# Second feed-forward product of a hybrid diffusion block: tokens on the output's partitions, weights as the moving side

## The chip, the cores and the metric

The kernel runs on one core of one Trainium2 chip. The metric is the device time of one execution in microseconds (us). A core has engines that work side by side and wait for each other through semaphores: TensorE (PE, matrix products; its weight loads are listed apart as PEld), VectorE (DVE), ScalarE (ACT), GpSimd (POOL) and SyncE (SP, which here only issues transfers). Transfers (DMAs) run on queues of their own, which share 16 DMA engines. [...]

In a matrix product one operand is *stationary*: PE loads a block of 128 x 128 of it ahead of the matmul. The other one is *moving*: up to 512 columns of it stream through. The stationary operand's columns become the partitions of the result, the moving operand's columns its free dimension.

## The reference

One layer of a diffusion block over 512 tokens of width D = 1024, with 256 context tokens beside them, in float32, and a last RMSNorm:

```python
h_lat = modulate(x, norm1_g[l], sh1, sc1)
h_ctx = modulate(ctx, norm1_g[l], csh1, csc1)
o_lat, o_ctx = token_mixer(h_lat, h_ctx, ...)      # Mamba-2 SSD and windowed attention, merged, one output product
x = x + gt1 * o_lat
x = x + gt2 * conv_ffn(modulate(x, norm2_g[l], sh2, sc2), w_up[l], ffn_conv_w[l], ffn_conv_b[l], w_down[l])
return rmsnorm(x, final_g)

def conv_ffn(h, w_up, conv_w, conv_b, w_down):
    u = dwconv_centred(h @ w_up, conv_w, conv_b)   # w_up: 1024 x 5632; 3 taps along the tokens
    a, b = u[..., :D_FF], u[..., D_FF:]            # D_FF = 2816
    return (jax.nn.silu(a) * b) @ w_down           # w_down: 2816 x 1024
```

`modulate` is an RMSNorm over the channels, times (1 + scale), plus shift; shift, scale and the gate gt2 are vectors over the channels. The change touches what comes after the first residual sum (called x1 below): the second feed-forward product `@ w_down` ("down"; `h @ w_up` is "up"), the second residual sum, the last RMSNorm and the store of the result.

## The kernel before, in words

**Layout.** The kernel keeps channels on partitions: x1 stands as eight tiles of 128 channels x 512 tokens (`x1[c // 4][:, c % 4, :]`), and so do the normalized input, the up product's tiles and the result, which is stored as (channels, tokens) and turned on the host. A per-channel vector (the gate, a norm's weight) is thus one value per partition; a sum over channels is one over partitions.

**Precision.** Each float32 operand is split into a high and a low part (`hi`, `lo`), and each product is three matmuls: hi by hi, hi by lo, lo by hi. Weights are split on the chip: `split` (L177) copies to `whi` on ACT (L178) and subtracts on DVE to `wlo` (L179).

**Weights.** The program is a list of steps that `run` (L201) goes through; each names the weight pieces it needs, and `run` calls `load` a fixed number of pieces ahead. `load_raw` (L164) issues the transfer on SP's queue into one of three buffers `wraw` of 128 x 1024 (for half of the down pieces into the larger `dnraw`). `weave` (L213) strews the steps of one list between those of another. A planner sets the order of the instructions on each engine by estimated times and priorities, except where a `manual_schedule` block or a `keep_in_program_order` holds it.

**Second norm and up product.** The tokens are handled in two halves of 256. In the first of 22 up steps (`up_step`, L1906) the normalized tiles of a half are made one after the other by `norm2_k` (L1844: DVE scales into `tb`, ACT makes the high part `mh`, DVE or POOL the low part `ml`), and PE uses each (L1915) as soon as it is there. In every later step `gemm` (L228, L229, L231) makes two tiles of 128 channels x 512 tokens, 24 matmuls of 512 moving tokens each; `up_first` and `up_second` apply the convolution and the gated SiLU into `F["x"]` (`fx`), and `f_sums` (L1867) makes the operands of the down product's first two products.

**Down product.** Down is a 2 x 2 block product by the scheme with seven products: the blocks are two halves of the tokens and two of the output channels, and the even and odd tiles of the 2816 inner channels. Its operands are sums and differences of blocks. Those of the weights are made by POOL's accumulating transfers in DRAM early on (`SUMS`, `DSUMS`); those of the activations by `f_sums`. Each product j has an operand `fs` of 11 tiles (DK = 11) x 256 tokens, hi and lo, and four column blocks q of 128 output channels. `product` (L1963) makes one: 11 x 3 matmuls (L1971 to L1973) with a weight block of 128 x 128 stationary and 256 tokens moving, on a half PSUM bank. Its weights come as two pieces of 768 and 640 columns. Products 0, 2 and 4 accumulate in one pair of banks (`mis`), the others in banks of their own (`acc`).

**Beside it.** `down_step` (L1977) adds what a column block gives to x1 at once: `x_add` (L1949) is one DVE operation with the gate as a per-partition value, `half_square` (L1954) squares a finished tile on ACT and adds it to `q3` on DVE. In products 1 to 5 `f_split` (L1863) splits the operand of the next product.

**The last product and the end.** `down_last` (L2014) handles the last RMSNorm. The sum over channels is made on PE (`rms_sums`, L271), then come DVE (L281) and POOL's power (L282), and the root is spread over the partitions by PE transposes (`rms_spread`, L288). For one half of the tokens (`u` = 1) this stands inside the last product's matmuls (`root`, `spread`, `early`), and `finish` (L2018) scales and stores it there; for the other half it comes after the last matmul (L2072, L2073, then `rms_root`, `rms_spread`, `finish`).

The order of steps is in the list handed to `run`: after `close_c1` come the 22 up steps, woven with what is left of the modulation's steps, then `down_step(j, q)` for 6 products of 4 column blocks, then `down_last()`.

Of the kernel before, what the change touches and what calls it, by code (L numbers as in the profile page):

```python
# [44 lines left out]
def tile_hybrid_layer(  # L45
# [25 lines left out]
    win_d: bass.AP,  # L71
    sel_d: bass.AP,
# [67 lines left out]
    DPARTS = ((0, 6), (6, DK - 6))  # L140
    DSUMS = {i: dpool.tile([4, P, DK * P], F32, name="dsum%d" % i) for i in (1, 2, 4, 5)}
    for q in range(4):
        for j, t in enumerate((wdn[0, q], DSUMS[1][q], DSUMS[2][q], wdn[1, q], DSUMS[4][q], DSUMS[5][q], wdn[3, q])):
            for u, (k0, n) in enumerate(DPARTS):
                src["dn", (4 * j + q) * 2 + u] = t[:, k0 * P : (k0 + n) * P], n * P

    SUMS = []
    for j, first_, more in (
        (4, wdn[0], wdn[2]), (1, wdn[2], wdn[3]), (2, DSUMS[4], wdn[3]), (5, DSUMS[2], wdn[1]),
    ):  # L150
        SUMS += [(DSUMS[j][q], first_[q], {}) for q in range(4)]
        SUMS += [(DSUMS[j][q], more[q], dict(accum_op=ALU.add, max_dma_last_dim=DK * P)) for q in range(4)]
# [11 lines left out]
    def load_raw(key):  # L164
        a, n = src[key]
        if key[0] == "dn" and key[1] >= 4 and key[1] % 2:
            if "dnraw" not in F:
                F["dnraw"] = hpool.tile([P, 5, 6 * P], F32, tag="hlh", name="dnraw")
            r = F["dnraw"][:, key[1] // 2 % 5, :]
        else:  # L170
            r = wpool.tile([P, 1024], F32, tag="raw", name="wraw", bufs=3)
# [11 lines left out]
    def load(key):  # L183
# [7 lines left out]
        if key[0] == "dn" and key[1] % 4 > 1:  # L191
            if "dnw" not in F:
                F["dnw"] = hpool.tile([P, 2, 2, 6 * P], F32R, tag="hll", name="dnw")
# [54 lines left out]
    a1 = cpool.tile([P, KT, 2], F32, name="a1")  # L248
    s1 = cpool.tile([P, KT, 2], F32, name="s1")
# [9 lines left out]
    tt_d = dpool.tile([64, 4], F32, name="tt_d")  # L259

# [138 lines left out]
    ssq = hpool.tile([P, L], F32, name="ssq")  # L399
# [1541 lines left out]
    q3 = hpool.tile([P, L], F32, tag="q2", name="q3")  # L1941

    ng2 = cpool.tile([P, 4], F32, name="ng2")
# [5 lines left out]
    def x_add(c, u, a, ps):  # L1949
        x = x1[c // 4][:, c % 4, HALF[u]]  # L1950
        g = ng2[:, c - 4 : c - 3] if a < 0 else mod2[:, 24 + c : 25 + c]
        V.scalar_tensor_tensor(x, ps, g, x, ALU.mult, ALU.add)

    def half_square(c, u):  # L1954
        x, q = x1[c // 4][:, c % 4, HALF[u]], q3[:, HALF[u]]
        if c % 4 == 0 and (c, u) in ((0, 0), (4, 1)):
            S.activation(q, x, AF.Square)
        else:
            sq = tmp("tc")[:, :HL]
            S.activation(sq, x, AF.Square)  # L1960
            V.tensor_tensor(q, q, sq, ALU.add)

    def product(j, q, w, ps, st, after={}):  # L1963
        s = F["s"][(0, 1, 0, 1, 0, 1, 0)[j]]
        with tc.manual_schedule(engines={mybir.EngineType.PE}):
            for u, (k0, n) in enumerate(DPARTS):
                wh, wl = w[u]
                for k in range(n):
                    c, h, l = slice(k * P, (k + 1) * P), s[:, 0, k0 + k, :], s[:, 1, k0 + k, :]
                    en = k0 + k == DK - 1  # L1970
                    T.matmul(ps, wh[:, c], h, start=st and k0 + k == 0, stop=False, skip_group_check=True)  # L1971
                    T.matmul(ps, wh[:, c], l, start=False, stop=False, skip_group_check=True)  # L1972
                    T.matmul(ps, wl[:, c], h, start=False, stop=en, skip_group_check=True)  # L1973
                    if k0 + k in after:
                        after[k0 + k]()

    def down_step(j, q):  # L1977
        def fn(*w):
            if j == 0 and q == 0:
                V.tensor_scalar_mul(ng2, mod2[:, 28:32], -1.0)  # L1980
# [198 lines left out]
```

## Time and profile before

| | |
|---|---|
| median of 3 runs | 1230.14 us (1230.03 to 1231.89) |
| profiled execution, its own time | 1229.7 us |
| span from first to last instruction | 1227.9 us |
| granted TensorE clock, mean | 0.998 |
| first and last matmul of the down product start | 1106.5 and 1218.4 us |
| DMA packets | 104,761, with 206.35 MB |

The page of a profile gives, in this order: busy time, share of the span and number of instructions of each engine; the span in 40 slices, a digit of tenths of busy time for each engine; the DMA queues; the chain of work that ended last, followed back from the end; and the costliest groups of instructions. A group's row names line, engine, operation, output <- inputs, their shapes and the count, then total busy time and the mean of one in ns, then the idle time just ahead of them with what ended it. A row of the timeline has the start in us, the length, engine, line, operation and shapes; in brackets, how long the engine was idle ahead of it and what released it. Matmuls overlap in the pipe: a matmul's length is longer than its distance to the next one.

### The profile page before, as it was taken

Reading aid. Unit: us, or ns where it says so; the run is one execution under the profiler, and the core shown is the slowest. Engines: PE = TensorE matmul, PEld = TensorE weight load, DVE = VectorE, ACT = ScalarE, POOL = GpSimd, SP = SyncE. Lnnn points to the kernel's source line nnn. Section 1 sums busy time; section 2 is a strip of 40 time slices with the busy share of each in tenths; the row PEclk is TensorE's granted clock in tenths of the full one; section 3 lists DMA queues with packets and bytes.
Section 4 is the critical chain, followed back from the end, with each engine's and each line's share of the span. In section 5 each row is a group of like instructions: output and inputs, shape, how many; then the busy total and the mean of one; then the engine's idle time right before and its main releaser. Section 6 shows DMA issues by size and latency. Waiting matters only on the chain.

```text
span 1227.9 us, 18427 instructions
## 1 busy us (share of the span) xinstructions
PE 1218.8 (99%) x6790; PEld 1021.5 (83%) x6790; DVE 921.4 (75%) x1518; ACT 686.7 (56%) x1289; POOL 170.0 (14%) x177
## 2 busy tenths in 40 slices
PE   9999999999999999999999999999999999999997
PEld 6798888888878878778777778889988888889997
DVE  5857788888555598797896767676777777778785
ACT  5658788787545367485574763223634434345662
POOL 0000120100000043252542540000200000000000
PEclk9999999999999999999999999999999999999999
DMA  9755799744754446356366568676233433337662
GB/s 368 256 136 185 156 257 259 161 153 129 177 158 143 129 103 183 120 120 196 106 169 208 164 212 282 206 242 206 58 116 104 136 114 110 117 102 236 187 178 82
DMA packets 104761, 206.35 MB, mean 168 GB/s; under 512 B 8928, under 2 KB 52768, under 8 KB 104416
## 3 DMA queue, kind: packets, MB, share of 16 engines
q1 hardware_dynamic: 94736, 181.32, 48.1%
q0 software_dynamic: 8960, 23.07, 8.2%
q8 instruction: 53, 0.87, 0.3%
q10 hardware_dynamic: 976, 0.79, 0.2%
q14 instruction: 36, 0.29, 0.1%
HBM read 182.54 MB, written 40.17 MB: 181 GB/s over the span
## 4 chain that ended last, share of the span: by engine, by line
PE 99%; DVE 0%; ACT 0%; issue 0%; POOL 0%; DVEq 0%; ACTq 0%; POOLq 0%
PE acc L228 20%; PE acc L231 20%; PE acc L229 20%; PE score L946 3%; PE po L995 3%; PE pt L982 2%; PE mis L568 2%; PE mis L1599 2%; PE mis L1492 2%; PE acc L1971 2%; PE acc L1973 2%; PE acc L1972 2%; PE mis L1607 1%; PE mis L1972 1%; PE mis L1971 1%; PE mis L1973 1%
## 5 line engine op out<-in xcount | busy, mean ns | idle before, releaser
L178 ACT CAST whi<-wraw 128x1024 fp32r<-128x1024 f32 (+3 forms) x118 | 120.0, 1018 | 156.4 <-PE acc L229 112.1
L228 PE MATMUL acc<-hlh,whi 128*128 128x512 f32 x472 | 194.2, 411 | 0.0
L179 DVE TENSOR_TENSOR wlo<-wraw,whi 128x1024 fp32r<-128x1024 f32 (+3 forms) x118 | 142.9, 1211 | 66.6 <-ACT whi L178 63.4
L229 PE MATMUL acc<-hll,whi 128*128 128x512 f32 x472 | 185.0, 392 | 0.0
L231 PE MATMUL acc<-hlh,wlo 128*128 128x512 f32 x472 | 184.8, 392 | 0.0
L228 PE MATMUL acc<-mh,whi 128*128 128x512 f32 x368 | 143.3, 390 | 0.0
L229 PE MATMUL acc<-ml,whi 128*128 128x512 f32 x368 | 143.2, 389 | 0.0
L231 PE MATMUL acc<-mh,wlo 128*128 128x512 f32 x368 | 143.2, 389 | 0.0
L231 PEld LDWEIGHTS acc<-hlh,wlo 128*128 128x128 f32 x472 | 88.6, 188 | 19.5
L228 PEld LDWEIGHTS acc<-hlh,whi 128*128 128x128 f32 x472 | 88.8, 188 | 18.0 <-issue 3.1
L229 PEld LDWEIGHTS acc<-hll,whi 128*128 128x128 f32 x472 | 89.0, 188 | 17.3 <-issue 2.4
L231 PEld LDWEIGHTS acc<-mh,wlo 128*128 128x128 f32 x368 | 69.1, 188 | 14.5
L229 PEld LDWEIGHTS acc<-ml,whi 128*128 128x128 f32 x368 | 69.1, 188 | 14.3
L228 PEld LDWEIGHTS acc<-mh,whi 128*128 128x128 f32 x368 | 69.1, 188 | 14.2
L282 POOL TENSOR_TENSOR rs<-ms,phalf 128x2 f32<-128x2 f32 (+1 forms) x5 | 4.8, 955 | 463.2 <-DVE ms L281 463.2
L1380 DVE SCALAR_TENSOR_TENSOR ta<-acc,half,ta 128x511 f32<-128x511 f32 (+1 forms) x66 | 43.9, 665 | 27.8 <-ACT ta L1379 27.6
L955 DVE CUSTOM_DVE_ANT_0 p<-score,winm,nsink 128x512 f32<-128x512 f32 (+1 forms) x64 | 51.9, 810 | 15.4 <-PE score L946 13.9
L1379 ACT ACTIVATE ta<-acc,half 128x512 f32<-128x512 f32 (+1 forms) x66 | 46.8, 709 | 22.3 <-PE acc L231 21.0
L962 ACT ACTIVATE p<-p,mneg 128x512 f32<-128x512 f32 (+1 forms) x64 | 49.7, 777 | 15.4 <-DVE mneg L955 14.8
L228 PE MATMUL acc<-hch,whi 128*128 128x256 f32 x176 | 54.7, 311 | 0.0
L990 DVE TENSOR_TENSOR ptl<-pt,pth 128x512 fp32r<-128x512 f32 x72 | 47.5, 685 | 8.5 <-ACT pth L986 7.7
L784 DVE SCALAR_TENSOR_TENSOR tm<-wraw,csil,tm 128x512 f32<-128x512 f32 x56 | 44.4, 793 | 12.4 <-DMA wraw<-wm 11.3
(414 smaller groups left out, 3160.6 us busy)
## 6 DMA issues: line engine op xcount, KB each, us to landing
wraw<-wup SPq DMA_DIRECT2D x44, 512.0 KB, 3.5
dsum<-wdn POOLq DMA_DIRECT2D x24, 704.0 KB, 8.6
fb<-cs_d SPq DMA_DIRECT2D x32, 512.0 KB, 6.5
wraw<-wm SPq DMA_DIRECT2D x32, 512.0 KB, 3.7
wraw<-wx SPq DMA_DIRECT2D x24, 512.0 KB, 3.6
wm<-wm SPq DMA_DIRECT2D x16, 512.0 KB, 8.4
wraw<-wz SPq DMA_DIRECT2D x16, 512.0 KB, 4.1
wraw<-wos SPq DMA_DIRECT2D x16, 512.0 KB, 4.6
```

The lines of the kernel that those rows point to most:

```text
L178: S.copy(hi[:, :n], r[:, :n])
L179: return V.tensor_tensor(lo[:, :n], r[:, :n], raw(hi[:, :n]), ALU.subtract)
L228: T.matmul(ps, wh, xh[:, k0 + k, :], start=a, stop=False)
L229: T.matmul(ps, wh, xl[:, k0 + k, :], start=False, stop=False)
L231: T.matmul(ps, wl, xh[:, k0 + k, :], start=False, stop=b)
L784: V.scalar_tensor_tensor(acc, r[:, u * 512 : u * 512 + 512], sc, acc, ALU.mult, ALU.add)
L946: T.matmul(ps[:, o : o + len(z) * P], Q[h][:, b * P : (b + 1) * P], k[:, j, z[0] * P : (z[-1] + 1) * P], start=v == 0 and o % 512 in (0, P ...
L955: V.tensor_tensor_reduce(p[:, :w], d["ps"][i][:, o0 : o0 + w], m, op0=ALU.add, op1=ALU.min, scale=1.0, scalar=nsink[:, h : h + 1], accum_o ...
L962: S.activation(p, p, AF.Exp, bias=d["mneg"][:, i : i + 1], scale=-1.0, accum_out=d["den"][:, i : i + 1])
L990: V.tensor_tensor(d["ptl"][x], d["pt"][x], raw(d["pth"][x]), ALU.subtract)
L1379: S.activation(o[:, :n], ps[:, :n], AF.Identity, scale=hcol(base_w, stride + i), bias=hcol(base_b, i))
L1380: V.scalar_tensor_tensor(o[:, 1:n], ps[:, 0 : n - 1], hcol(base_w, i), o[:, 1:n], ALU.mult, ALU.add)
```

## The change

The down product is turned: its result has tokens on the partitions. Of an activation operand `fs` a block of 128 tokens is stationary, and 512 weight columns (half of the output channels) are moving. Each of the seven products then has two blocks of 128 tokens instead of four of 128 channels, with 11 x 3 matmuls each on a full PSUM bank. The scheme, its sums and the number of weights are the same.

- **Weights.** `wdn` is packed so that for each inner tile its 512 columns are next to each other. A product's weights are loaded as six pieces (DU = 6), five of 1024 columns (two inner tiles) and one of 512, instead of eight of 768 or 640. `DSUMS` has the same layout; its transfers stay 24 + 8 of the old sizes. `dnraw` has 4 buffers of 1024 instead of 5 of 768.
- **x1 is turned through DRAM.** `x1_turn(c)`, eight times: a DVE transpose within blocks of 32 x 32 of x1's tile c into a buffer `te`, then four SP transfers that write it to `x1_d` (tokens, channels) in DRAM, each of 512 runs of 32 values (128 bytes). `x1_load` then reads x1 back as four tiles of 128 tokens x 1024 channels. These steps are woven into the up steps.
- **Row tiles.** The gate and the last norm's weight now run along the free dimension. `row_tiles` makes tiles of 128 x 512 of them by broadcasting transfers from DRAM (`g2_d`, written there first in pieces of 4 bytes, and `fg_d`, a new input).
- **Sums.** `x_add` and `half_square` go. The functions in `BESIDE_DOWN` take their place, each at one step (j, u): copies of PSUM on ACT, sums on DVE, multiplication by the gate and the residual sum on POOL, all 512 wide. Squares are summed along the free dimension by ACT's `accum_out`; the sums, spreads and transposes of the last norm on PE go.
- **The end.** The last step of the last product takes two weight pieces and does block 0's nine matmuls, then block 1's nine. `near_last` and `near_out` do the rest for each block; the scaled rows are stored as (tokens, channels), so nothing is turned on the host.

```diff
     DK = NFF // 2
-    DPARTS = ((0, 6), (6, DK - 6))
+    HC = D // 2
+    DU = (DK + 1) // 2
...
+    for j, t in enumerate((wdn[0], DSUMS[1], DSUMS[2], wdn[1], DSUMS[4], DSUMS[5], wdn[3])):
+        for u in range(DU):
+            n = min(2, DK - 2 * u) * HC
+            src["dn", DU * j + u] = t[:, 1024 * u : 1024 * u + n], n
...
-                F["dnraw"] = hpool.tile([P, 5, 6 * P], F32, tag="hlh", name="dnraw")
+                F["dnraw"] = hpool.tile([P, 4, 1024], F32, tag="hlh", name="dnraw")
...
+    def x1_turn(c):
+        def fn():
+            t = tmp("te")
+            V.transpose(t, x1[c // 4][:, c % 4, :])
+            for a in range(4):
+                o = x1_d[:, c * P + 32 * a : c * P + 32 * a + 32].rearrange("(f i) j -> i f j", i=32)
+                nc.sync.dma_start(o, t[32 * a : 32 * a + 32, :].rearrange("i (f j) -> i f j", j=32))
+        return [], fn
+
+    def x1_load():
+        F["xt"] = []
+        for h, tag in enumerate(("hch", "hcl")):
+            x = hpool.tile([P, 2, D], F32, tag=tag, name="xt")
+            F["xt"].append(x)
+            for i in range(2):
+                r = 256 * h + P * i
+                nc.sync.dma_start(x[:, i, :], x1_d[r : r + P, :])
...
+    def row_tiles():
+        V.tensor_copy(g2c[:, 0:4], mod2[:, 24:28])
+        V.tensor_scalar_mul(g2c[:, 4:8], mod2[:, 28:32], -1.0)
+        nc.sync.dma_start(g2_d.rearrange("(c p) -> p c", p=P), g2c)
+        tiles = [hpool.tile([P, HC], F32, tag=t, name="row" + t) for t in ("q2", "ssq", "rbc4")] + [tmp("tm")]
+        rows_["g"], rows_["f"] = tiles[:2], tiles[2:]
+        for i in range(2):
+            z = slice(HC * i, HC * i + HC)
+            nc.sync.dma_start(rows_["f"][i], fg_d[z].partition_broadcast(P))
+            nc.sync.dma_start(rows_["g"][i], g2_d[z].partition_broadcast(P))
...
+    def square_sum(h, i, col_, x):
+        sq = tmp("ta")[:, : x.shape[-1]]
+        S.activation(sq, x, AF.Square, scale=1.0 / 32.0, accum_out=ss[:, 2 * h + i, col_ : col_ + 1])
+
+    def scale_add(x, y, g, h, i, c):
+        G.tensor_tensor(x, y, rows_["g"][c], ALU.mult)
+        G.tensor_tensor(xq(h, i, c), xq(h, i, c), x, ALU.add)
...
+    def near_last(i):
+        ps = F["ps", 6][i]
+        for b, z in enumerate(HALF):
+            t = tmp("ta")[:, :HL]
+            V.tensor_tensor(t, ps[:, z], rows_["g"][1][:, z], ALU.mult)
+            x = xq(0, i, 1, z)
+            V.tensor_tensor(x, x, t, ALU.add)
+            square_sum(0, i, 1 + b, x)
+        F["near", i] = mean_root(0, i, ss[:, i, 1:2], ss[:, i, 2:3], ss[:, i, 0:1])
+
+    def near_out(i):
+        rs, r = F["near", i], P * i
+        S.activation(F["p1"][i], F["p1"][i], AF.Copy, scale=rs)
+        S.dma_start(out[r : r + P, 0:HC], F["p1"][i])
+        for z in HALF:
+            x = xq(0, i, 1, z)
+            V.scalar_tensor_tensor(x, x, rs, rows_["f"][1][:, z], ALU.mult, ALU.mult)
+            nc.sync.dma_start(out[r : r + P, HC + z.start : HC + z.stop], x)
+
+    BESIDE_DOWN = {
+        (0, 0): row_tiles, (1, 0): first_kept, (2, 0): fifth_kept, (3, 0): far_sum, (4, 0): near_sum, (4, 4): near_done,
+        (5, 0): lower_sums, (5, 5): lower_done, (6, 0): upper_sums, (6, 3): lambda: (upper_done(), far_roots()),
+    }
...
-                    T.matmul(ps, wh[:, c], h, start=st and k0 + k == 0, stop=False, skip_group_check=True)
-                    T.matmul(ps, wh[:, c], l, start=False, stop=False, skip_group_check=True)
-                    T.matmul(ps, wl[:, c], h, start=False, stop=en, skip_group_check=True)
...
+                wh, wl = (x[:, k % 2 * HC : k % 2 * HC + HC] for x in w[k // 2])
+                h, l = s[:, 0, k, tok], s[:, 1, k, tok]
+                st, en = k == 0 and (j == 0 or not chain), k == DK - 1
+                T.matmul(ps, h, wh, start=st, stop=False, skip_group_check=True)
+                T.matmul(ps, l, wh, start=False, stop=False, skip_group_check=True)
+                T.matmul(ps, h, wl, start=False, stop=en, skip_group_check=True)
...
+        tail = j == 6 and u == DU - 2
...
+            if tail:
+                far_out()
+                for i in TWO:
+                    product(j, i, w, ks)
+                with tc.manual_schedule(engines={mybir.EngineType.DVE, mybir.EngineType.Activation}):
+                    for f in (near_last, near_out):
+                        for i in TWO:
+                            f(i)
+                return
+            for k in ks:
+                for i in TWO:
+                    product(j, i, w, (k,))
...
-        + weave([up_step(t) for t in range(NFF)], msteps[24:])
-        + [down_step(j, q) for j in range(6) for q in range(4)]
-        + down_last(),
+        + weave(weave([up_step(t) for t in range(NFF)], msteps[24:]), [([], lambda: None)] * 6 + [x1_turn(c) for c in range(8)] + [x1_rows] + [([], lambda: None)] * 7)
+        + [down_step(j, u) for j in range(7) for u in range(DU - (j == 6))],
```

223 lines of the change are left out of this document (96 added, 127 removed).

## The prediction

> **What bounds the kernel now.** I read the page first (busy time, slices, chain), then three stretches of the last 360 us, then the spacing of single matmuls.
>
> ```profile
> span 1227.9 us, 18427 instructions
> PE 1218.8 (99%) x6790; PEld 1021.5 (83%) x6790; DVE 921.4 (75%) x1518; ACT 686.7 (56%) x1289; POOL 170.0 (14%) x177
> PE 99%; DVE 0%; ACT 0%; issue 0%; POOL 0%; DVEq 0%; ACTq 0%; POOLq 0%
> 870.00:990.00 120.00, 120.00 (x557) 100.27 (x557) 92.55 (x137) 51.95 (x76) 2.95 (x4) 1.00 0.36 109
> 990.00:1107.00 117.00, 117.00 (x522) 96.95 (x521) 88.48 (x127) 48.09 (x67) 0.00 (x0) 1.00 0.35 111
> 1107.00:1228.00 121.00, 112.96 (x940) 112.43 (x939) 92.26 (x150) 65.76 (x101) 2.81 (x4) 0.98 0.57 173
> ```
>
> PE carries the whole chain, at full clock. The columns of a stretch are its length, then busy time and count for PE, weight loads, DVE, ACT and POOL, then clock, DMA share and GB/s. The up product (to 1107) has PE full, DVE at 77% and the DMA engines at 36%. The second (down) product has PE full until 1218.6 and a tail of some 9 us without matmuls. So a microsecond counts only if it leaves PE's stream or the tail, or makes PE wait. The profiled execution took 1229.7 us, its span 1227.9; the median of the runs shown is 1230.14, 0.4 above it.
>
> **Part 1: half as many, twice as wide matmuls.** Before, each of 7 products has 4 column blocks of 11 k by 3 matmuls: 924, of 256 moving tokens. After, 2 token blocks by 11 by 3: 462, of 512 moving weight columns. The streamed columns are equal; only the cost per instruction can differ.
>
> ```profile
> 1106.52 0.36 PE L1971 MATMUL mis<-fs,whi 128*128 128x256 f32 x1
> 1114.26 0.28 PE L1972 MATMUL mis<-fs,dnw 128*128 128x256 f32 x1
> 1118.94 0.28 PE L1972 MATMUL mis<-fs,dnw 128*128 128x256 f32 x1
> 1218.42 0.28 PE L1973 MATMUL acc<-fs,dnw 128*128 128x256 f32 x1
> ...
> 1099.81 0.39 PE L231 MATMUL acc<-mh,wlo 128*128 128x512 f32 x1
> 1103.89 0.39 PE L231 MATMUL acc<-mh,wlo 128*128 128x512 f32 x1
> ...
> 1099.81 0.19 PEld L228 LDWEIGHTS acc<-mh,whi 128*128 128x128 f32 x1
> ```
>
> From 1114.26 to 1118.94 lie 39 steps of 256 columns: 0.120 us each. From 1099.81 to 1103.89 lie 18 steps of 512: 0.2267 each. Two narrow ones cost 0.240, one wide one 0.2267: 13.3 ns saved per pair. The wide matmul needs one 0.19 us weight load in 0.2267, as the up product does, so alternating stationary operands is nothing new. First to last start is 111.90 us, with the last step 112.02; 924 x 0.120 = 110.88, so the eight sums (L271) and two spreads (L288) inside the stream cost 1.14. After: 462 x 0.2267 = 104.73, and no sums on PE. **Gain 7.3 us.**
>
> The Trainium skill, "TensorE: Matmul & The Clock Gate", section Back-to-back issue gap, gives N/2.4 + 2.5 ns when warm: 109.2 and 215.8 ns here. By it a pair would save 2.5 ns and part 1 only 1.2 + 1.1 us. This trace has 120.0 and 226.7, so 13.3 ns of fixed cost at either width; the measured spacing decides.
>
> **Part 2: eight block transposes on DVE.** No row has one. Nearest are 512-wide DVE operations; bounds are 0.42 (256 wide) and 1.22 us (1024 wide). I take 0.69.
>
> ```profile
> 869.01 0.87 DVE L1847 SCALAR_TENSOR_TENSOR tb<-x,a,mis 128x256 f32<-128x256 f32 x2 [0.74 <-issue]
> 870.07 0.48 DVE L1854 SCALAR_TENSOR_TENSOR ml<-tb,mod,mh 128x256 fp32r<-128x256 f32 x1 [0.18 <-ACT mh L1848]
> 883.38 0.69 DVE L1897 TENSOR_TENSOR fx<-ta,tc 128x512 f32<-128x512 f32 x1
> 885.63 0.42 DVE L1873 TENSOR_TENSOR fx<-fx 128x256 f32<-128x256 f32 x1
> 900.02 1.22 DVE L179 TENSOR_TENSOR wlo<-wraw,whi 128x1024 fp32r<-128x1024 f32 x1 [1.31 <-ACT whi L178]
> ...
> 872.55 0.74 POOL L1852 TENSOR_TENSOR ml<-ta,mh 128x256 fp32r<-128x256 f32 x1 [0.85 <-ACT ta L1851]
> ...
> 873.34 0.39 PE L1915 MATMUL acc<-ml,whi 128*128 128x256 f32 x1
> ...
> 898.94 1.05 ACT L178 CAST whi<-wraw 128x1024 fp32r<-128x1024 f32 x1 [0.95 <-PE acc L229]
> ```
>
> In the built order of the changed kernel DVE does not keep them to the steps where they are written. The first two stand in the second RMSNorm: one ahead of the second root's small operation (where DVE waits 0.96 us anyway), the next between the scaling of the second half's first two tiles (869.01) and their low parts (870.07). There DVE, ACT and POOL feed PE just in time: POOL's piece ends at 873.29 and PE's matmul, with the longer 0.39, starts at 873.34. So the second transpose moves PE's end of this stage by its length, and the order's shuffle of two scalings adds about 0.15. **Loss 0.85 us**, between 0 and 1.4. The other six meet PE's lead: a weight split starts when PE lets a buffer go (898.94), is done at 901.24, and is used only after the next 24 matmuls, 5.44 us later: 3.1 us to spare. They cost nothing, as long as DVE does not wait for transfers.
>
> **Part 3: 32 transfers of 128 bytes a piece, and the reload.** Each transpose is written out by four transfers of 512 pieces: 16,384 packets. Six transposes reuse a buffer, so DVE waits until the transfers of the transpose two before have landed, with weight splits queued behind. SP issues these between the weight loads, each later load queues behind, and the reload (four times 512 KB) waits on SP for the last of them.
>
> ```profile
> q1 hardware_dynamic: 94736, 181.32, 48.1%
> q10 hardware_dynamic: 976, 0.79, 0.2%
> ...
> DMA packets 2722, 1.99 MB, mean 249 GB/s; under 512 B 68, under 2 KB 2481, under 8 KB 2722
> q1 hardware_dynamic: 2722, 1.99, 90.1%
> ...
> wraw<-wup SPq DMA_DIRECT2D x44, 512.0 KB, 3.5
> ```
>
> The first two lines are the page's queues, the middle two 368 to 376 us, where loads of 512-byte pieces fill the engines. There 2,722 packets took 0.901 x 16 x 8 = 115 us of engine time: 42 ns each. The issuing queue q10 writes results of some 0.8 KB at 0.002 x 16 x 1227.9 / 976 = 40 ns; scaled by bytes, 128 of them would be 6 ns. The whole of q1 averages 100 ns. So 6 to 100 ns; I take 35 to 42, nearest the full stretch. 16,384 x 42 / 16 = 43 us of all engines. By the built order they lie between 865 and 940 us, among 15 weight loads of 0.36 x 120 / 26 = 1.66 us (26 loads in 870 to 990): 25 us, so 50 us are free. It fits, 86% filled. Weights have time: a load is issued three splits ahead, 16 us, minus the split: about 11 us before its cast, against 3.5 to land. Later transposes may wait 1 to 2 us for landings, inside the 3.1. **Cost nothing**, cover gone at 49 ns; beyond it 1 us for each ns.
>
> **Part 4: the sums.** Splits go from 56 pieces (768 or 640 wide) to 42 (1024 or 512), with the same columns; PE's step is 12 x 0.2267 = 2.72 us against about 1.2 of DVE for a split. 16 POOL operations of 512 are new; six per product at 1.5 us are 9 of its 15 us. The tightest place is the last product. DVE there waits for POOL's root ahead of the split for its fifth weight piece.
>
> ```profile
> L1610 POOL TENSOR_TENSOR dx<-dx,te 128x512 f32<-128x512 f32 x16 | 23.6, 1477 | 68.0 <-DVE te L1601 68.0
> ```
>
> From the product's start: sum 1.1, four POOL operations to 7.0, root to 7.8, scaling to 8.6, split to 9.8 us. PE needs it at 4 x 2.72 + 0.45 = 11.3. Cost nothing, with 1.5 us to spare. Row loads and gate (1,024 pieces of 4 bytes) block SP about 4 us at the product's start; the pieces behind are due 15 us later.
>
> **Part 5: the tail.**
>
> ```profile
> 1218.74 0.61 DVE L2072 SCALAR_TENSOR_TENSOR x<-acc,ng,x 128x128 f32<-128x128 f32 x2 [2.80 <-PE acc L1973]
> 1219.19 0.51 ACT L2073 ACTIVATE tc<-x 128x128 f32<-128x128 f32 x2 [3.84 <-DVE x L2072]
> 1220.19 0.16 DVE L281 TENSOR_SCALAR ms<-mis 128x2 f32<-128x2 f32 x1 [0.84 <-PE mis L271]
> 1220.50 0.70 POOL L282 TENSOR_TENSOR rs<-ms,phalf 128x2 f32<-128x2 f32 x1 [11.95 <-DVE ms L281]
> 1221.72 2.44 DVE L2032 SCALAR_TENSOR_TENSOR x<-x,vec,mis 128x256 f32<-128x256 f32 x6 [1.37 <-PE mis L288]
> L2034 SPq DMA_DIRECT2D out<-x x7: 333/372/399, 1212.8 to 1224.3; - x7
> DMA to landing us min/median/max: 1.7/2.2/2.6
> ```
>
> Before, from the last matmul's start S = 1218.42: last issue at S + 5.9, end at S + 9.5. After, block 0 stops nine matmuls (2.04) earlier. DVE needs four 256-wide operations (0.42 to 0.48) per block: block 0 to S + 0.35, square and mean to S + 1.0, block 1 to S + 3.0, square and mean to S + 3.7, root to S + 4.5, two scalings to S + 5.5, issue S + 5.6. The trips through PE go, the sums of two blocks on one DVE come. 1 MB leaves in the tail as before. **0, within -1 and +1.**
>
> Sum: 1229.7 - 7.3 + 0.85 + 0 = 1223.2, and 0.4 for the median: **1223.6 us**.
>
> **Rivals.** (a) Small packets are slower than 49 ns: the engines fill up between 865 and 940, weights and DVE's reused buffers come late, PE waits in the up product. Ahead of PE stands only the 11 us of lead. If a piece shorter than the normal 512 bytes is both read and written at its target, at 42 ns each way, it costs 84 ns: 35 x 1.02 = 36 us, 1259 us. It turns the sign at 58 ns (9 us). For it: no row has such a packet, and the stage is 86% full at 42. Against: the 0.8 KB writes at 40 ns show no heavy fixed cost. The Trainium skill, "DMA: Bandwidth & Descriptors", section Specifications, says below 512 B the engine does read-modify-write; no run here shows it. (b) Transfers fit, but waits eat most of the gain: landings exceed the 3.1 us at some transposes and the last product's split comes late; 1 to 5 us, 1227. For it: DVE at 77%, 86% full engines. Against: each wait has its own cover. (c) The width saves little because the moving side now is freshly split weights: by 2.5 ns a pair, 1223.6 + 5.0 = 1228.6. Against it is the up product's 512 spacing; its stationary side holds weights, though, and no row has weights moving here at 512. This is also the result of the skill's gap rule named above.
>
> **How the numbers follow.** Forecast 60%, (a) 22%, (b) 14%, (c) 4%. The forecast's own range is 1221 to 1226 (tail and norm bounds). 0.2%, 2.5 us, is about what a measurement of this kernel tells from no change. Faster: the forecast, two thirds of (b), 0.70; same: the rest of (b), (c), 0.08; slower: (a), 0.22. The range 1221 to 1238 leaves out the far half of (a) and little below.
>
> **What would show it.** Right: 462 matmuls 0.227 apart without gaps, about 105 us from first to last; PE full from 880 to 1106 and no DVE wait for x1's transfers over 3 us; a packet mean under 49 ns between 865 and 940; 9 to 10 us after the last matmul. Wrong: idle PE in the up product with casts waiting for DMA; small issues that take longer than 1.5 us each in a row on SP; PE idle ahead of the last product's fifth weight piece.

## The result, and the profile after

The changed kernel takes 1225.79 us (median of 6 runs, 1225.30 to 1226.77), the kernel before in the same runs 1232.02 (1230.03 to 1232.19): a ratio of 0.9956 (of the means), 95% interval 0.9943 to 0.9968. It is faster, by 6.2 us in the medians and 5.5 in the means; forecast were 6.5, from 1230.14 to 1223.6. The six runs of the kernel before lie at 1230.0 to 1230.1 or at 1231.9 to 1232.2. The profiled execution of the changed kernel took 1225.3 us with a span of 1223.5, 4.4 below that of before. That is less than 6.2, since the kernel before was profiled at the low end of its own times (1229.7); the stages below are compared in the profiles.

From the page of the changed kernel: its engines, its queue of loads, the chain.

```profile
span 1223.5 us, 17434 instructions
PE 1211.2 (99%) x6310; PEld 994.7 (81%) x6310; DVE 921.3 (75%) x1479; ACT 682.3 (56%) x1275; POOL 201.4 (16%) x193
...
q1 hardware_dynamic: 111280, 186.83, 49.0%
...
PE 95%; DVE 2%; issue 1%; POOL 1%; ACT 1%; DMA 0%; POOLq 0%; DVEq 0%; ACTq 0%
```

The chain was 99% PE and is 95% now: somewhere it leaves PE. The same three stretches as in the prediction (length; busy time and count of PE, weight loads, DVE, ACT, POOL; clock, DMA share, GB/s) show where POOL came in:

```profile
870.00:990.00 120.00, 119.84 (x556) 99.89 (x556) 95.61 (x143) 52.44 (x76) 2.95 (x4) 1.00 0.52 144
990.00:1107.00 117.00, 117.00 (x518) 96.89 (x517) 89.19 (x130) 47.36 (x65) 0.00 (x0) 1.00 0.38 117
1107.00:1224.00 117.00, 106.11 (x468) 86.90 (x466) 85.94 (x103) 62.10 (x88) 31.50 (x20) 0.98 0.60 180
```

In the up product the DMA share moved most (0.36 to 0.52), DVE has 3.1 and 0.7 us more, and PE is full but for 0.16 us. In the down product POOL works 31.5 us where it worked 2.8. The timeline of PE there, with the first matmul, the one place where PE stands still, and the last matmul:

```profile
1107.50 0.49 PE L2104 MATMUL mis<-whi,fs 128*128 128x512 f32 x1
...
1125.09 0.39 PE L2106 MATMUL acc<-dnw,fs 128*128 128x512 f32 x1
...
1196.95 0.39 PE L2105 MATMUL acc<-dnw,fs 128*128 128x512 f32 x1
...
1197.40 0.39 PE L2104 MATMUL acc<-whi,fs 128*128 128x512 f32 x1
...
1197.93 0.49 PE L2106 MATMUL acc<-wlo,fs 128*128 128x512 f32 x1
1199.66 0.50 PE L2104 MATMUL acc<-whi,fs 128*128 128x512 f32 x1 [1.24 <-DVE te L2048]
...
1213.97 0.39 PE L2106 MATMUL acc<-wlo,fs 128*128 128x512 f32 x1
```

From 1125.09 to 1196.95 lie 317 steps: 0.2267 us each. But from 1197.93 to 1199.66 lie 1.73 us, 1.50 too many. PE waits for a DVE sum, `te` of `upper_sums` (L2048), which reads product 5 from a bank of PSUM (the memory that matrix products accumulate into) that product 6's second block takes over: the pool `acc` has three banks, and products 1, 3, 5 and 6 take them in turn. The stages, in the profiles:

| us | before | after |
|---|---|---|
| from the sums of the first half's root (PE, `te`) to down's first matmul | 865.85 to 1106.52: 240.67 | 866.21 to 1107.50: 241.29 |
| down, first to last matmul | 111.90 | 106.47 |
| last matmul to the end of the span | 9.48 | 9.53 |

The first stage begins with these rows, of before and after:

```profile
865.85 0.58 PE L271 MATMUL mis<-rmsc,te 128*128 128x1 f32 x4
```

```profile
866.21 0.58 PE L276 MATMUL mis<-rmsc,te 128*128 128x1 f32 x4
```

The rest of the difference, 0.36 us, is older: the same matmuls already lie 0.2 to 0.4 us later from 6 us on, and the first instruction of `x1_turn` stands at 864.96.

### The profile page after: what moved, and what is told of

It reads as the page before. It is cut to its first block, busy times and chain, and to the rows that moved or that the text cites. A ratio compares the mean times of both kernels' runs of the same rounds, so it can differ in the third digit from the quotient of the medians.

```text
span 1223.5 us, 17434 instructions
## 1 busy us (share of the span) xinstructions
PE 1211.2 (99%) x6310; PEld 994.7 (81%) x6310; DVE 921.3 (75%) x1479; ACT 682.3 (56%) x1275; POOL 201.4 (16%) x193
## 4 chain that ended last, share of the span: by engine, by line
PE 95%; DVE 2%; issue 1%; POOL 1%; ACT 1%; DMA 0%; POOLq 0%; DVEq 0%; ACTq 0%
PE acc L231 20%; PE acc L234 20%; PE acc L232 20%; PE score L951 3%; PE po L1000 3%; PE pt L987 2%; PE mis L573 2%; PE mis L1604 2%; PE mis L1497 2%; PE mis L1612 1%; PE mis L2104 1%; PE mis L2106 1%; PE mis L2105 1%; PE acc L1070 1%; PE acc L1071 1%; PE acc L1072 1%
## 5 line engine op out<-in xcount | busy, mean ns | idle before, releaser
L181 ACT CAST whi<-wraw 128x1024 fp32r<-128x1024 f32 (+1 forms) x115 | 120.2, 1046 | 152.3 <-PE acc L232 102.7
L182 DVE TENSOR_TENSOR wlo<-wraw,whi 128x1024 fp32r<-128x1024 f32 (+1 forms) x115 | 145.7, 1267 | 66.7 <-ACT whi L181 64.3
L162 POOL DMA_DIRECT2D dsum<-wdn x24 | 25.4, 1144 | 193.0 <-DVE wlo L1084 171.7
L1499 POOL TENSOR_TENSOR st<-st,eT 128x512 f32<-128x512 f32 x24 | 29.1, 1214 | 166.0 <-ACT st L1516 152.0
```

Source lines behind the costliest of these rows:

```text
L181: S.copy(hi[:, :n], r[:, :n])
L182: return V.tensor_tensor(lo[:, :n], r[:, :n], raw(hi[:, :n]), ALU.subtract)
```

## The experiments

All are made from the changed kernel. "Stream" is the time from down's first matmul to its last.

**The width alone (e1_narrow).**

```diff
-                T.matmul(ps, h, wh, start=st, stop=False, skip_group_check=True)
-                T.matmul(ps, l, wh, start=False, stop=False, skip_group_check=True)
-                T.matmul(ps, h, wl, start=False, stop=en, skip_group_check=True)
+                for v, (a, b) in enumerate(((h, wh), (l, wh), (h, wl))):
+                    for z in HALF:
+                        T.matmul(ps[:, z], a, b[:, z], ...)
```

> The changed kernel with each matmul of 512 moving columns issued as two of 256 with the same stationary block; nothing else is changed. If the gain is the fixed cost of a matmul (13.3 ns for each pair, from the two spacings of the kernel before), the down product's stream, 106.5 us from first to last start in the changed kernel, becomes 106.5 + 462 x 0.0133 = 112.6, and the span goes from 1223.5 to about 1229.6: slower than the kernel before by about 1.7 us. If the width saves only 2.5 ns a pair (rival c) and the gain came from the sums taken off PE, the stream becomes 107.6 and the span 1224.7.

Measured: ratio to before 0.9994 (0.9985 to 1.0004); stream 111.13, span 1227.6, nearer to the first theory than to rival (c). The stall of 1.5 us is missing here; 923 steps at 0.120 make 110.8 of the 111.1. At product 6, four matmuls (0.12 apart) make a row:

```profile
1202.27 0.64 PE L2106 MATMUL acc<-whi,fs 128*128 128x256 f32 x4
1202.75 0.40 PE L2106 MATMUL acc<-wlo,fs 128*128 128x256 f32 x2
1203.19 0.74 PE L2106 MATMUL acc<-whi,fs 128*128 128x256 f32 x4
```

The second block starts 0.44 after the last row, 0.2 later than without a wait. So the fixed 13.3 ns per pair are shown, 6.1 us in all; without them the changed kernel can't be told from the one before. The 0.8 us by which this stream is still below that of before are of the size of the sums and spreads that left PE (1.14), less these 0.2. The expected 112.6 for the stream was too high by the stall: the slower stream gives DVE the time it lacks.

**Another bank for product 6 (e2_bank).**

```diff
-                F["ps", j] = F["A"] if j in (0, 2, 4) else [accb() for _ in TWO]
+                F["ps", j] = F["A"] if j in (0, 2, 4) else [(misb if j == 6 else accb)() for _ in TWO]
```

> The changed kernel with the two PSUM banks of product 6 taken from the pool of five (mis) instead of the pool of three (acc). In the changed kernel PE stands still for 1.5 us at product 6's second block, released by a DVE sum (te) that reads product 5's first bank. If the shared bank is what PE waits for, that gap of 1.73 us between starts becomes 0.23. But the split of product 6's fifth piece, which ends 11.8 us after the product's start and is due after 11.3, then comes late by about 0.5 us: PE waits there, and the span falls by 1.0, to 1222.5. Rival: PE waits for the weights' splits anyway (DVE is behind with them), and the gap only moves to the next piece: the span stays within 0.3 of 1223.5.

Measured: ratio 0.9952 (0.9937 to 0.9967), span 1224.1, stream 107.50. From PE's timeline:

```profile
1123.50 0.50 PE L2106 MATMUL acc<-dnw,fs 128*128 128x512 f32 x1 [0.53 <-DVE dnw L182]
...
1198.53 0.50 PE L2106 MATMUL mis<-wlo,fs 128*128 128x512 f32 x1
1198.86 0.39 PE L2104 MATMUL mis<-whi,fs 128*128 128x512 f32 x1
...
1212.39 0.50 PE L2106 MATMUL mis<-wlo,fs 128*128 128x512 f32 x1 [0.88 <-DVE wlo L182]
```

The bank was what PE waited for: block 1 now starts 0.33 after block 0's third matmul. But the wait turned up further on: 0.3 at 1209.85 and 1.05 at 1212.39, where PE needs the low parts of the last two pieces. And a new one of 0.7 stands at 1123, in product 1, which the bank has nothing to do with.

**The squares later in the program (e3_square_later).**

```diff
-        (5, 0): lower_sums, (5, 5): lower_done, (6, 0): upper_sums, ...
+        (5, 0): lower_sums, (6, 0): upper_sums, (6, 1): lower_done, ...
```

> The changed kernel with the squares of lower_done moved from step (5, 5), ahead of product 6's first casts, to step (6, 1), behind upper_sums. In the changed kernel ACT waits 3.6 and 4.0 us in these squares for POOL's sums; the casts of product 6's first pieces stand behind them on ACT, their low parts on DVE behind the casts, and the sum that frees PE's bank behind these on DVE. If this chain is the cause, the casts come some 2 to 3 us earlier, DVE's sum starts as soon as product 5's first block is ready, PE's gap of 1.73 falls to 0.23 to 0.5, and the fifth piece's split is earlier too: span about 1222.0. Rival: DVE is simply full there (its operations take 1.6 to 1.9 us instead of 1.2 while POOL works beside it), and the gap stays above 1.2: span 1223.3.

This one missed: in the trace the squares stand where they stood; the planner had put them back, and the instructions of every engine are in the order of the changed kernel. So it is the changed kernel once more, with a ratio of 0.9965 (0.9952 to 0.9978), a span of 1226.3 and a stream of 109.34. The gap at product 6 is 1.74 as before; 2.6 us more are lost in product 1. ACT and PE there, in this execution:

```profile
1123.33 1.04 ACT L181 CAST dnw<-wraw 128x1024 fp32r<-128x1024 f32 x1 [6.72 <-DMA wraw<-dsum]
```

```profile
1124.42 0.50 PE L2104 MATMUL acc<-dnw,fs 128*128 128x512 f32 x1 [1.76 <-ACT dnw L181]
...
1125.68 0.50 PE L2106 MATMUL acc<-dnw,fs 128*128 128x512 f32 x1 [0.53 <-DVE dnw L182]
```

In the changed kernel's own profile the same cast started at 1118.92, 3.7 us before its matmul. Between 1105 and 1125 that profile has, of the queue (packets, MB, share) and of its issues (KB, us to landing):

```profile
q1 hardware_dynamic: 2160, 3.58, 86.2%
...
wraw<-dsum SPq DMA_DIRECT2D x3, 512.0 KB, 7.3
dnraw<-dsum SPq DMA_DIRECT2D x2, 512.0 KB, 9.1
...
rowq<-g_d SPq DMA_DIRECT2D x1, 256.0 KB, 4.5
...
g_d<-g2c SPq DMA_DIRECT2D x1, 4.0 KB, 11.5
```

The gate's 4 KB, in 1,024 pieces of 4 bytes, take 11.5 us to land, and SP stands from 1114.1 to 1123.8 at the read that waits for it. The weights in flight beside it take 7.3 us here and 11.4 in e3.

**The transposes out of the norm (e4_turn_held).**

```diff
+            F["gated"] = V.tensor_tensor(F["x"][t % 2][:, t // 2, :], a, b, ALU.mult)      # up_second
...
+            turn = V.transpose(t, x1[c // 4][:, c % 4, :])
+            tc.add_manual_dep(turn.ins, F["gated"].ins.name, BEHIND, ...)
```

> The changed kernel with each block transpose of x1 held behind the gated product of the up step before it, so that none stands in the second RMSNorm. Theory: the two transposes there cost PE what its matmuls came later from 866 to 883 us than in the kernel before, 0.98 less the 0.35 that the executions differed already = 0.6 us: span 1222.9. The transfers start some 20 us later and stay hidden. Rival: the shift comes from the planner's other order of that stage, or is not caused by the transposes, and the span stays at 1223.5; or the turned tiles come too late or the transposes now push splits in the up steps, and PE shows idle time there.

Measured: ratio 0.9954 (0.9938 to 0.9971), span 1225.1. From the sums (866.62) to down's first matmul (1107.31) it takes 240.69, as before the change (240.67): the 0.6 us were the two transposes in the norm (all eight stand between 959 and 1036 us here). The span isn't lower, since this execution lost 1.6 us in product 1, as e3 did.

**The gate in larger pieces (e5_gate_turn).**

```diff
-        nc.sync.dma_start(g2_d.rearrange("(c p) -> p c", p=P), g2c)
+        V.transpose(t[:, 32:64], t[:, 0:32])          # the gate's 8 columns stand in t[:, 0:8]
+        for a in range(4):
+            nc.sync.dma_start(g2_d.rearrange("(c p) -> c p", p=P)[:, 32 * a : 32 * a + 32], t[32 * a : 32 * a + 8, 32:64])
```

> The changed kernel with the gate written to DRAM in 32 pieces of 128 bytes (after a block transpose of a 128 x 32 tile on DVE) instead of 1,024 pieces of 4 bytes. Theory: in the changed kernel that write of 4 KB takes 11.5 us to land, SP stands at the read behind it for 10 us, and the weight pieces of product 1 that share the DMA engines with it land after 7 to 12 us instead of 3.5 to 4; PE waits there between 0 and 2.7 us, another amount in each execution. Then the write lands in under 4 us, these pieces in under 6, PE has no gap over 0.4 us in product 1, and the time is 1224.5 to 1225.5 in every run, with a smaller spread. Rival: the engines are simply full of weights at the start of the down product (0.86 of their time), the pieces come as late without the small ones, and PE waits as before.

Measured: ratio 0.9944 (0.9929 to 0.9959); four runs from 1224.17 to 1224.36; no gap in product 1. SP goes on at 1118.65, 4.7 us after the first write instead of 11.5, and the weights beside it land after 4.8 (median; 7.3 before). Between 1105 and 1125:

```profile
q1 hardware_dynamic: 1806, 5.13, 80.2%
...
wraw<-dsum SPq DMA_DIRECT2D x5, 512.0 KB, 4.8
dnraw<-dsum SPq DMA_DIRECT2D x4, 512.0 KB, 5.9
```

The rival, full engines alone, is out: they move 5.13 MB there at a share of 0.802, the changed kernel 3.58 MB at 0.862. By this 50 us of engine time per MB, the changed kernel spends 0.862 x 320 - 3.58 x 50 = 97 us more than its bytes need, 95 ns for each of the 1,024 pieces. But the pieces did not take this time themselves. The traces also hold every single packet: those of 4 bytes have a median of 9 ns there, and it is the weights' packets of 4,096 bytes that grow, to a mean of 304 ns against 191 here (median 159 in both). Most of the long ones start from 1116 us on, when most of the small ones are through. So the small pieces hold up the loads behind them. Whether by their number, their length or their common target of 4 KB is not shown, since this edit changes all three.

The times of the runs do not show what the edit is worth. e8_twice (below), on the same chip and with the small pieces, has runs from 1224.08 to 1224.62 and no wait in product 1. And of the 0.9 us by which the span lies below the changed kernel's, 0.8 are in the tail (8.7 for 9.5), behind the last scaling, which the edit doesn't touch: the last four stores on SP land after 2.3 us instead of 2.9. What does show it is the cover, over all profiled executions of 512-wide products. In the eight with the small pieces the cast of product 1 starts 1.1 to 5.8 us before its matmul, and PE waits in five (0.2 to 2.6 us); in the three without them (here, e7_all, e9_scale_dve) it starts 5.7 to 6.2 us before, and PE waits in none.

**The order in the last product (e6_order).** With e2's banks, and:

```diff
+            tc.add_manual_dep(q.ins, F["cast"].ins.name, BEHIND, ...)     # squares of lower_done and upper_done
+            tc.add_manual_dep(o.ins, F["low"].ins.name, BEHIND, ...)      # scalings of far_out
```

> The changed kernel with product 6 on banks of the larger pool, and three groups of instructions held by dependencies: the squares of lower_done behind the cast of product 6's third piece, those of upper_done behind the cast of its last piece, and far_out's scalings behind the split of its last piece. (Moving the first squares in the program alone changed nothing: the planner put them back.) Theory: POOL's sums, of 1.3 to 2.3 us each, hold ACT's squares, these hold casts, these hold DVE's splits, and PE waits at product 6's second block or, with another bank, at its fifth piece; then both waits go, the stream from product 6's first matmul to the last one is 64 x 0.2267 + 0.3 = 15.2 us instead of 16.6 (from 1197.4 to 1213.97), and the span falls by 1.4 us if nothing else differs. Rival: the far half's sums, roots and scalings, now later, run into the tail: the last matmul starts 1.4 us earlier, but the end stays where it was.

Measured: ratio 0.9957 (0.9942 to 0.9972), span 1224.8. Both sides were right: PE has no gap over 0.3 us in product 6 (0.55 us are lost in product 1), so POOL, ACT and DVE were the chain; but the far half's scalings run into the tail. It takes 10.8 us from the last matmul's start instead of 9.5.

**All three (e7_all).** e4, e5 and e6 together.

> The changed kernel with the gate's transpose, the order held in the last product, its other banks, and the block transposes of x1 held out of the second RMSNorm. If the three losses (0.6 in the norm, 0 to 2.7 in product 1, 1.5 in product 6) are independent, the span is 1223.5 - 0.6 - 1.4 = 1221.5 us, the stream of the down product 105.1, and the median some 1223.3. Rival: they share slack, and what one gives the next takes: not below 1223.

Measured: ratio 0.9945 (0.9930 to 0.9960), span 1223.3, stream 104.68 as expected, but the tail 10.6: the rival of e6 again. The last scalings on DVE start 4.5 us after the last matmul (1217.18 against 1212.68), in the changed kernel 3.2 (1217.15 against 1213.97). The median, 1224.31, is that of e5_gate_turn and e8_twice on the same chip (1224.29 and 1224.47): the three mends together bring nothing that the runs show.

**x1 written twice (e8_twice).**

```diff
+                for d in (x2_d, x1_d):
+                    o = d[:, c * P + 32 * a : c * P + 32 * a + 32].rearrange("(f i) j -> i f j", i=32)
+                    nc.sync.dma_start(o, ...)
```

> The changed kernel with each of the 32 transfers of x1's turned tiles issued twice, the second time into another DRAM tensor: 16,384 more pieces of 128 bytes, with the same buffers waiting for both. By the share of the DMA engines in the changed kernel (0.503 of 65 us against 0.328 before, for 14,448 small packets) a piece takes 12.6 ns of an engine; then 12.9 us more of all engines are still covered, the share there rises to about 0.65, and the time stays within 0.5 us. By the price that the prediction took (42 ns) it would be 43 us more where some 30 are free: 10 us longer or more. Rival within the first: the queue that issues them, at 0.3 to 0.8 us each, gets 13 us more to do, the weights behind come late, and PE waits for a microsecond or two in the up product.

Measured: ratio 0.9945 (0.9928 to 0.9961), span 1222.8; 16,896 more packets (the 16,384 pieces and 16 for each transfer), and no cost that the runs show. As a test of full engines it is inconclusive, since the planner issued the second copies after 940 us and the window of the first ones is as it was. As a price it holds: the queue's share rises from 49.0% to 50.2%, (0.502 x 1222.8 - 0.490 x 1223.5) x 16 / 16,896 = 14 ns for a packet; the median of the 128-byte packets themselves is 13.

**The sum off POOL (e9_scale_dve).** e7_all, and in `upper_sums`:

```diff
-            scale_add(c, c, 0, 1, i, 0)
+            V.tensor_tensor(c, c, rows_["g"][0], ALU.mult)
+            G.tensor_tensor(xq(1, i, 0), xq(1, i, 0), c, ALU.add)
```

> The kernel with all three mends (e7_all), and the gate's multiplication in upper_sums moved from POOL to DVE. In e7_all the stream of the down product fell to 104.7 us, but the tail from the last matmul's start to the end of the span grew from 9.5 to 10.6: POOL's four sums (2.2 us each beside DVE) end at 1208.4, so the far half's four scalings run until 1212.4 on DVE and block 0's sums start 1.3 us later against the last matmul than in the changed kernel. Theory: with two of the four sums gone from POOL, the far half's scalings end before 1211, the tail is 9.5 again, and the span is 1.0 below e7_all's for the same start of the down product: from that start to the end 104.7 + 9.5 = 114.2 us, where the changed kernel has 116.0 and e7_all 115.3. Rival: DVE is full there, the two more operations of 0.7 us push the splits of the last two pieces, and PE waits for them.

Measured: 1223.21 us (1223.14 to 1223.84), ratio 0.9935 (0.9923 to 0.9948). It is the fastest of all, 2.1 us below the changed kernel beside it (below). Its span is 1222.1, its stream 104.66, and the last scalings start 3.7 us after the last matmul, 0.8 earlier than in e7_all. From down's start to the end it takes 114.6 us (the tail 9.9 of them), where e11_again takes 116.0; 114.2 were expected. With the 0.6 of the norm these are 2.0 us; the spans differ by 1.3, since e9's execution is 0.7 later at 866 already. DVE was not too full: PE has no gap. Its last matmul and the last scalings, from PE's and DVE's timelines:

```profile
1212.17 0.39 PE L2116 MATMUL mis<-wlo,fs 128*128 128x512 f32 x1
```

```profile
1215.91 1.80 DVE L2097 SCALAR_TENSOR_TENSOR xt<-xt,rs,tm 128x256 f32<-128x256 f32 x4
```

**Pieces of 32 bytes (e10_quarter).**

```diff
+                for b in range(4):
+                    o = x1_d[:, c * P + 32 * a + 8 * b : c * P + 32 * a + 8 * b + 8].rearrange("(f i) j -> i f j", i=32)
+                    nc.sync.dma_start(o, t[32 * a : 32 * a + 32, :].rearrange("i (f j) -> i f j", j=32)[:, :, 8 * b : 8 * b + 8])
```

> The changed kernel with each transfer of a turned tile cut into four, of 8 values each: 65,536 pieces of 32 bytes instead of 16,384 of 128. If a piece has a fixed price of 12.6 ns, these are 826 us of engine time, 52 us of all 16, in some 75 us that had 35 free: they spill over into the up product's later steps, and the time grows by 0 to 3 us. If the price goes by bytes, nothing changes. If the price rises as pieces get shorter, towards the 95 ns that the gate's 4-byte pieces cost (the share of the engines from 1105 to 1125, with them and without them), it is up to 390 us of all engines: the turned tiles are not ready at product 4, PE waits, and the time is 100 us longer or more.

Measured: ratio 0.9961 (0.9946 to 0.9977), span 1222.8; PE's gaps are those of the changed kernel but for 0.2 us in product 1, and the up product has none. The packets between 865 and 930 us, here, in the changed kernel and before:

```profile
DMA packets 45982, 7.74 MB, mean 119 GB/s; under 512 B 44440, under 2 KB 44440, under 8 KB 45976
...
q1 hardware_dynamic: 45976, 7.67, 65.7%
```

```profile
DMA packets 15989, 8.13 MB, mean 125 GB/s; under 512 B 14448, under 2 KB 14448, under 8 KB 15984
...
q1 hardware_dynamic: 15984, 8.06, 50.3%
```

```profile
q1 hardware_dynamic: 1739, 6.34, 32.8%
```

So 44,440 small packets took (0.657 - 0.328) x 16 x 65 = 342 us, 7.7 ns each, and 14,448, most of them of 128 bytes, took 182 us, 12.6 ns each. The single packets in the traces agree, with medians of:

| bytes | 4 | 32 | 128 | 512 | 2,048 | 4,096 |
|---|---|---|---|---|---|---|
| ns | 9 | 7 | 13 | 27 | 84 | 159 |

Neither a fixed price nor one by bytes alone fits: it is about 8 ns and 0.037 ns for each byte. No price rises for short pieces.

**The changed kernel again (e11_again).**

> The changed kernel once more, beside the others on the same chip: 0.9956 of the kernel before, with a gap of 1.73 us at product 6's second block in every execution, and in product 1 a wait of 0 to 2.7 us that differs between executions. e9_scale_dve is then 1.5 to 2.5 us below it if the theory holds.

Measured: ratio 0.9956 (0.9944 to 0.9969), 1225.31 us (1225.17 to 1229.12); the gap at product 6 is 1.74. In this execution there was no wait in product 1.

## Why the prediction was right, and where it was not

The median of 1225.79 lies in the range, and the change of -6.2 us is near the -6.5 forecast. Part of that is luck. In the profiles the span fell by 4.4 where the working has 7.3 - 0.85 = 6.45: 1.5 of the rest is the stall in product 6, 0.36 is there before the changed part begins, and the last 0.2 is the sum of small items. The runs make up for it, since those of the kernel before have their median at 1232.02 now and had it at 1230.14 in the three that the prediction had.

- **Part 1, the width: right.** 0.1200 and 0.2267 us were expected, 0.1200 and 0.2267 measured; e1_narrow takes the gain away by undoing the width alone. The Trainium skill ("TensorE: Matmul & The Clock Gate", Back-to-back issue gap) gives N/2.4 + 2.5 ns as the gap of an isolated matmul. By that, e1_narrow's stream would have been 107.6; it was 111.1. The measurement decides.
- **Part 2, the transposes in the norm: right in kind, a little large.** 0.62 us for 0.85 taken, at 0.70 for a transpose (0.69 taken); e4_turn_held has them back.
- **Part 3, the small transfers: hidden, as forecast, but the price was three times too high.** PE is full in the up product, and no wait stands ahead of any of the eight transposes. Taken were 35 to 42 ns for a packet, measured 12.6. The stage was thus nowhere near full (0.52), and rival (a) had no ground. (By the prediction's own figures its sign would have turned at 49 + 6.5 = 55 ns, not at 58.) The stretch taken for nearest has larger packets: its 2,413 of 512 bytes took 30 ns on average, and 241 of 2,048 and 4,096 bytes bring the mean to 42. And the prediction's "no row has such a packet" holds for the rows alone. The page before counts 8,928 packets under 512 bytes, and in that trace 128 each of 64, 192 and 224 bytes took 11 to 17 ns. The Trainium skill ("DMA: Bandwidth & Descriptors", Specifications) has read-modify-write below 512 bytes; what it would cost can't be told apart here, but pieces of 128 and 32 bytes got cheaper, not dearer.
- **Part 4 is the step that failed, twice.** First, "row loads and gate block SP about 4 us": it is 10 us, for the gate's write takes 11.5 us to land, and it holds up the weights beside it as well. The cover named behind it, that the pieces behind are due 15 us later, is used up: the cast starts 3.7 us before its matmul in one execution, and PE waits 1.8 for it in another of the same program. This makes 0 to 2.6 us, and 0 in the three executions without the small pieces (e5, e7, e9). Second, "six per product at 1.5 us": POOL's 16 operations of 512 columns take 1.81 on average (1167.8 to 1206.7), 1.3 alone and up to 2.3 beside DVE, and DVE's splits grow with them. The chain in the changed kernel, from the timelines of POOL, ACT and DVE:

```profile
1187.45 1.30 POOL L2000 TENSOR_TENSOR xt<-xt,tc 128x512 f32<-128x512 f32 x1
1188.70 2.29 POOL L2037 TENSOR_TENSOR xt<-xt,ta 128x512 f32<-128x512 f32 x1
1190.95 2.27 POOL L1999 TENSOR_TENSOR tc<-tc,rowssq 128x512 f32<-128x512 f32 x1
1193.30 1.61 POOL L2000 TENSOR_TENSOR xt<-xt,tc 128x512 f32<-128x512 f32 x1
```

```profile
1194.94 0.63 ACT L1996 ACTIVATE ta<-xt 128x512 f32<-128x512 f32 x1 [3.98 <-POOL xt L2000]
1195.58 1.04 ACT L181 CAST whi<-wraw 128x1024 fp32r<-128x1024 f32 x1
1196.52 1.05 ACT L181 CAST whi<-dnraw 128x1024 fp32r<-128x1024 f32 x1
```

```profile
1187.93 1.90 DVE L182 TENSOR_TENSOR wlo<-dnraw,whi 128x1024 fp32r<-128x1024 f32 x1
...
1196.65 1.23 DVE L182 TENSOR_TENSOR wlo<-wraw,whi 128x1024 fp32r<-128x1024 f32 x1 [1.18 <-ACT whi L181]
1197.79 1.22 DVE L182 TENSOR_TENSOR wlo<-dnraw,whi 128x1024 fp32r<-128x1024 f32 x1
1198.93 0.68 DVE L2048 TENSOR_TENSOR te<-acc,te 128x512 f32<-128x512 f32 x1
...
1207.30 0.75 DVE L2067 SCALAR_TENSOR_TENSOR xt<-xt,rs,rowrbc 128x512 f32<-128x512 f32 x1 [1.90 <-POOL rs L2058]
1207.97 1.22 DVE L182 TENSOR_TENSOR wlo<-wraw,whi 128x1024 fp32r<-128x1024 f32 x1
```

  POOL's sum holds ACT's square for 4 us; the casts of product 6 queue behind it, their low parts behind them, and behind these the sum that frees the bank. Product 5's first block was done at 1196.9 (its last matmul starts at 1196.49 and takes 0.39), and DVE came to it 2.0 later. The prediction looked for the tight place further on, at the fifth piece's split: worked out to end 9.8 us after the product's start and due after 11.3, it ended after 11.8 (1209.19). The sum ahead of it ended at 2.2 instead of 1.1, and POOL's four operations took 7.0 us instead of 5.9. It is hidden only because PE had lost 1.5 us before; e2_bank takes that cover away, and PE waits there. So the place was right as the next one, its 1.5 us of slack were not there.
- **DVE and POOL.** The first and the third split above have the same form, with 1.90 us beside POOL and 1.22 alone. The rows look like turns, not like a common slow-down: POOL's sum of 1187.45 takes its 1.30 and ends at 1188.75, DVE's split ends 1.08 after it (1189.83), and POOL's next operation 1.16 after the split (1190.99). DVE's sum from a bank is not lengthened: 0.68 alone (1198.93) and beside POOL (1200.66). The Trainium skill ("SBUF — State Buffer", Who interferes with whom) says that a DVE instruction with two inputs in SBUF contends with a GpSimd instruction that reads SBUF, for a shared port pair, which it calls an exclusive lock. The rows agree; had it been weighed, an operation of either engine would have been taken as its own time plus what is left of the other's.
- **Part 5, the tail: right,** 9.53 for 9.48. With the same last product it was 9.5 in e11_again and 8.7 to 8.8 in e5, e8 and e10; up to the last scaling these agree, and the last four stores land after 2.9 us or after 2.2 to 2.3. So it is not known better than that.
- **The rivals.** (a) and (c) are out by e10_quarter and e1_narrow. (b), waits that eat the gain, is half of what happened: 1.5 us in every profiled execution with the changed kernel's last product, and 0 to 2.6 more in product 1; not at the transposes, but in the down product.

What stays open: why the loads behind 1,024 pieces of 4 bytes take longer, where tens of thousands of 32 bytes do no harm (packets of 4,096 bytes take 215 ns on average in e10's stretch, 219 before); why they land after 7 us in one execution and after 11 in another; and what sets the landing of the last stores.

## What to carry to other kernels

On a full PE, count instructions as well as columns: 13 ns of fixed cost for each matmul is worth turning a product around, if what is turned with it lies under other work. Then look for the losses where the new helpers' output is waited for: not at the slow helper itself, but at the cast or split that stands behind a waiting instruction on the same engine, and at the bank that this holds. A wait that is removed shows the next one behind it (e2, e6, e7); only with the whole chain mended (e9) did the time move, by 2.1 us.

## What was not expected of the hardware

- Small packets on this queue took 13 ns at 128 bytes and 7 to 8 at 32, with no extra price for being short. But a write of 4 KB in 1,024 pieces of 4 bytes took 10.2 to 11.6 us to land, though the pieces took 9 ns each: the packets of the loads behind them grew, and 512 KB loads beside them landed after 7.3 to 11.4 us (medians), against 4.6 to 4.9 with 32 pieces of 128 bytes.
- DVE and POOL take turns where DVE's operation has both inputs outside PSUM: a DVE split of 1024 columns takes 1.22 us alone and up to 2.3 beside POOL, a POOL sum of 512 columns 1.3 alone and up to 2.3 beside DVE.
